# Gate columns of a float32 mixer projected on the split operands

## The chip, the cores and the metric

The kernel runs on one core of one Trainium2 chip. The metric is the device time of the whole program in microseconds (us); smaller is better. TensorE (PE in the profile) does the matmuls, VectorE (DVE), ScalarE (ACT) and GpSimd (POOL) the elementwise work, and SyncE (SP) issues the transfers. Each engine works through its own instructions in order, and waits where an operand is not there yet.

## The reference, cut to what matters

Two layers of a diffusion backbone on 2048 latent tokens and 256 context tokens of 1024 channels. Each layer normalises and modulates the tokens, projects them on one weight `w_in` with 4112 columns, and feeds two groups of heads: a gated convolution and a gated delta rule that is scanned in both directions. The last 16 of the 4112 columns are the ones of this document: 8 write gates and 8 decays (2 directions, 4 heads).

```python
mod_l = silu(c) @ w_mod + b_mod                    # shift, scale, gate
hl = rms_norm(xl, norm_w) * (1.0 + scale_l) + shift_l
pl = split_proj(to_scan_order(hl, col_major) @ w_in)   # D_PROJ = 8 * 512 + 16
...
beta = sigmoid(beta_logit)                         # columns 4096 to 4103
g = -exp(a_log) * softplus(alpha_in + dt_bias)     # columns 4104 to 4111
```

All of it is float32.

## The kernel before

**Tiling.** A layer has 18 tiles of 128 tokens, two of context and 16 latent, in five chunks: chunk 0 has two tiles (256 columns), chunks 1 to 4 four each (512 columns). Tokens lie along the free dimension of the matmuls and channels on partitions: `KT` = 8 blocks of 128 channels.

**Operands.** `prep` (L215) makes a chunk's operands, two channel blocks and 256 tokens at a time: PE transposes the normalised tokens (L225), ACT modulates them into the float32 tile `hf` (L231), DVE rounds that to float32r as `hi` (L235), and DVE or POOL takes the rest as `lo` (L236). The tiles are called `h` and `l`, for chunk 0 `hc` and `lc`. The weights are split in the same way into `whi` and `wlo` (L251, L253), and `project` (L278) forms each output as hi\*hi + lo\*hi + hi\*lo in float32r matmuls of 256 columns.

**Gate columns.** The 16 columns do not go that way. `ba_weights` loads them into a tile of 32 columns filled with zeros, `braw`, which has a buffer of its own. `prep` projects `hf` itself on them in full float32, one channel block at a time, each block `k` into one of four column groups of 32 of the array (L240):

```python
for dk in range(2):
    k = k2 + dk
    q = k % 4
    nc.tensor.matmul(acc[32 * q:32 * q + 32, o], bw[:, k, :], hf[:, dk, :], start=(k < 4), stop=(k >= 4))
```

So a chunk has 8 such matmuls for each 256 tokens, 144 in the two layers, and the bank `acc` is held from the first to the last block: a bank of `pt` (two buffers) for chunks 0 to 2, one of `pd` (three buffers, those of `project`) for chunks 3 and 4. `logits` copies the bank to SBUF (L324) and adds the four groups with a matmul per tile on `sel`, four identities on top of each other (L327). `gates` makes write gates and decays of them, which the scan (`delta`) needs.

**Start.** `mod_load` brings eight pieces of `w_mod`, 1 MB each, and `mod_piece` projects both condition vectors on them (L138, in column groups too) and gathers the groups (L143). `vectors` loads the layer's small per-channel vectors into the tile `rows` (L108 to L112), which PE turns channel-major (L114) into `par`. The modulation adds a column of `par` to each piece, so that no `hf` can be made before `par` is there. `rows` is a tile of the tag `dm`, which has three buffers that are handed out in the order of the program text; the tiles `cc` and `cth` of the prologue have that tag too.

**Order.** The text is recorded for all engines and then ordered by a scheduler that simulates the program and picks by priority; `urgent()` raises the priority of operands, weights and consumers by a fixed offset (`HP`). Each engine then runs its list in order. A matmul of the gates, of a scan step or of an operand's transposes stands among the projection's matmuls wherever the scheduler put it. `ba_weights` is not urgent.

## Time and profile before

| | us |
|---|---|
| median of 3 runs | 2879.31 |
| lowest and highest | 2876.04, 2884.07 |
| span of the profiled execution (first to last instruction) | 2868.8 |
| PE busy in it | 2740.4 (96%) |
| DVE, ACT, POOL busy | 1794.5, 1139.6, 1002.2 |

For the profiled execution the span alone is recorded; the median of the runs stands 10.5 us above it, which is the time of the program before its first and after its last instruction, and the spread of the runs. Busy times of PE count the union of records whose ends overlap, since matmuls are pipelined: what a matmul takes of PE is read from its start to the next one's start. A full float32 matmul leaves two records, a float32r matmul one.

### The profile page before, as it was taken

The numbers are of one execution on the slowest core, as the hardware profiler recorded it, in microseconds if no ns is written. First come the engines' busy times: TensorE is split into PE (matmuls) and PEld (weight loads), VectorE is DVE, ScalarE is ACT, GpSimd is POOL, SyncE is SP. The second block draws the span as 40 slices with busy tenths as digits, with TensorE's granted clock in tenths as the row PEclk, the third lists the DMA queues.
The fourth block names the chain that finished last, engine by engine and source line by source line (L and its number), as shares of the span: only waits on it lengthen the run. The fifth ranks groups of instructions, "written<-read, shape, count | busy, mean of one in ns | idle before, by whom it ended". The sixth has DMA issues, their size and how long they took to land. (4 is left out here: it accounts for less than half of the span.)

```text
span 2868.8 us, 62580 instructions
## 1 busy us (share of the span) xinstructions
PE 2740.4 (96%) x23671; PEld 2529.1 (88%) x23671; DVE 1794.5 (63%) x4677; ACT 1139.6 (40%) x2962; POOL 1002.2 (35%) x1354
## 2 busy tenths in 40 slices
PE   7999999999999999999999999999999998999998
PEld 5799899988988999997777998899999888899887
DVE  5686657576586585353246776675766765754765
ACT  3544453533534532232115444435335354322332
POOL 2332322333433343234444222313334333333443
PEclk9999999999999999999999999999999999999999
DMA  8844265553655553347757552545546556434654
GB/s 275 251 120 138 81 174 130 174 162 89 182 145 170 173 139 113 109 149 246 239 161 242 162 144 79 154 112 163 154 115 188 132 168 189 126 116 118 206 173 117
DMA packets 589449, 450.17 MB, mean 157 GB/s; under 512 B 105322, under 2 KB 527196, under 8 KB 589148
## 3 DMA queue, kind: packets, MB, share of 16 engines
q1 hardware_dynamic: 589148, 446.16, 53.7%
q8 instruction: 188, 3.08, 0.4%
q14 instruction: 113, 0.93, 0.1%
HBM read 326.35 MB, written 119.70 MB: 155 GB/s over the span
## 5 line engine op out<-in xcount | busy, mean ns | idle before, releaser
L278 PE MATMUL pd<-h,whi 128*128 128x256 f32 x4096 | 1206.6, 295 | 2.1 <-ACT whi L251 2.1
L278 PE MATMUL pd<-l,whi 128*128 128x256 f32 x4096 | 1207.2, 295 | 0.0
L278 PE MATMUL pd<-h,wlo 128*128 128x256 f32 x4096 | 1199.4, 293 | 0.5 <-POOL wlo L253 0.5
L278 PEld LDWEIGHTS pd<-h,whi 128*128 128x128 f32 x4096 | 795.2, 194 | 11.9 <-issue 6.6
L278 PEld LDWEIGHTS pd<-l,whi 128*128 128x128 f32 x4096 | 795.0, 194 | 9.0 <-issue 5.4
L278 PEld LDWEIGHTS pd<-h,wlo 128*128 128x128 f32 x4096 | 794.8, 194 | 6.4 <-issue 2.9
L253 POOL TENSOR_TENSOR wlo<-raw,whi 128x1024 fp32r<-128x1024 f32 (+1 forms) x148 | 341.3, 2307 | 382.3 <-ACT whi L251 349.7
L899 PE MATMUL pd<-who,yy 128*128 128x512 f32 x1088 | 350.7, 397 | 0.4 <-ACT who L841 0.4
L899 PEld LDWEIGHTS pd<-who,yy 128*128 128x128 f32 x1088 | 203.6, 189 | 48.0 <-ACT yy L874 2.9
L697 ACT ACTIVATE w<-pscan,cs 128x128 f32<-128x128 f32 x272 | 99.5, 367 | 291.8 <-DVE wk L692 209.1
L899 PE MATMUL pd<-wlo,yy 128*128 128x512 f32 x544 | 214.1, 393 | 0.0
L251 ACT CAST whi<-raw 128x1024 fp32r<-128x1024 f32 x148 | 154.7, 1045 | 97.4 <-PE pd L278 60.9
L501 POOL TENSOR_TENSOR nk<-nk,phalf 128x1 f32<-128x1 f32 x144 | 81.7, 567 | 225.2 <-DVE nk L500 205.8
L573 DVE TENSOR_TENSOR tmp<-L,X 64x31 f32<-64x31 f32 (+15 forms) x310 | 127.1, 410 | 39.9 <-DMA L<-blk 25.0
L388 ACT ACTIVATE pd<-y 128x512 f32<-128x512 f32 (+1 forms) x116 | 65.5, 565 | 213.0 <-DVE y L288 200.6
L686 DVE SCALAR_TENSOR_TENSOR r<-pscan,eg,rc 128x128 f32<-128x128 f32 x272 | 93.7, 346 | 76.7 <-PE pscan L684 74.5
L575 DVE TENSOR_TENSOR X<-X,tmp 64x31 f32<-64x31 f32 (+15 forms) x310 | 136.3, 440 | 5.6
L692 DVE TENSOR_SCALAR wk<-pscan,cs 128x128 f32<-128x128 f32 x272 | 93.5, 346 | 69.6 <-PE pscan L689 67.7
L875 POOL TENSOR_TENSOR yy<-ys,yy 128x512 fp32r<-128x512 f32 x68 | 89.9, 1323 | 125.4 <-ACT yy L874 118.3
L660 POOL TENSOR_TENSOR so<-so,mhalf 128x1 f32<-128x1 f32 x136 | 79.2, 590 | 142.5 <-DVE so L659 134.3
L703 DVE SCALAR_TENSOR_TENSOR Sn<-Sn,atot,pscan 128x128 f32<-128x128 f32 x240 | 82.0, 342 | 67.9 <-PE pscan L694 66.6
L874 ACT CAST yy<-ys 128x512 fp32r<-128x512 f32 x68 | 42.1, 619 | 198.2 <-DVE ys L867 136.8
(2212 smaller groups left out, 5317.3 us busy)
## 6 DMA issues: line engine op xcount, KB each, us to landing
raw<-in_w_in_dram SPq DMA_DIRECT2D x148, 512.0 KB, 4.8
rc<-rec_d SPq DMA_DIRECT2D x272, 256.0 KB, 3.1
rec<-rec_d SPq DMA_DIRECT2D x136, 192.0 KB, 2.6
wm<-in_w_mod_dram SPq DMA_DIRECT2D x24, 1024.0 KB, 7.3
rec_d<-y SPq DMA_DIRECT2D x96, 256.0 KB, 2.9
rows<-row_d SPq DMA_DIRECT2D x144, 128.0 KB, 4.1
rec_d<-rec SPq DMA_DIRECT2D x144, 128.0 KB, 4.0
ys<-y_d SPq DMA_DIRECT2D x68, 256.0 KB, 3.5
```

Of the source, the lines that this page charges most:

```text
L251: nc.scalar.copy(hi, raw)
L253: eng.tensor_sub(lo[:, k], raw[:, k], hi[:, k].bitcast(F32))
L278: nc.tensor.matmul(acc[:, c:c + CW], w[i][:, k, :], h[j][:, k, c:c + CW], start=(z == 0), stop=(z == len(passes) - 1))
L501: nc.gpsimd.tensor_tensor(nk[:, i:i + 1], nk[:, i:i + 1], phalf[:, 0:1], ALU.pow)
L573: nc.vector.tensor_tensor(t3, L3[:, j + 1:32, j:j + 1].to_broadcast([2 * nb, m, k]), X3[:, j:j + 1, 0:k].to_broadcast([2 * nb, m, k]), ALU ...
L575: nc.vector.tensor_sub(X3[:, j + 1:32, 0:k], X3[:, j + 1:32, 0:k], t3)
L686: nc.vector.scalar_tensor_tensor(r, p1[:, 0:128], eg[:, g, col], vn, ALU.mult, ALU.subtract)
L692: nc.vector.tensor_scalar(wk, p2[:, 0:128], cs[:, 5 + z0 + d, i:i + 1], None, ALU.mult)
L697: nc.scalar.activation(w, p2[:, 0:128], AF.Copy, scale=cs[:, z0 + d, i:i + 1])
L703: nc.vector.scalar_tensor_tensor(Sn, S, atot[:, g, col], p3[:, 0:128], ALU.mult, ALU.add)
L875: nc.gpsimd.tensor_sub(l_, yr, h_.bitcast(F32))
L899: nc.tensor.matmul(acc, yy[k // 4][:, k % 4, :], wo[k][part][:, cs_], start=(z == 0), stop=(z == 23))
```

## The change

The gate columns are split into two float32r parts like every other weight, and both parts stand side by side in one tile, `two`: for each block `k` 16 columns of the high part and 16 of the low one. Once the operands of a chunk are there, `logits` projects `hi` and `lo` on it, 8 blocks times 2 operands, all summed in one bank: 16 float32r matmuls a chunk, each over all tokens of the chunk. Their stationary operand is 96 columns wide: the 32 that count and the next 64 of the tile, whose sums land on partitions 32 to 95 and are not read. The matmul that gathers the parts then adds the 16 rows of the high part to the 16 of the low one (`both`), from 32 partitions. The bank is of `pd` for all chunks.

The raw columns are now loaded into a tile of tag `dm`. `csil`, the condition vectors, is stored more densely; its matmuls are as many and as large as before. Comments were dropped. Lines below the change stand a few numbers lower or higher: L276, L227 and L140 are the old L278, L225 and L138, L327 is the new projection, L332 the gather.

```diff
+        both = const.tile([32, 16], F32, name="both")
+        nc.vector.tensor_add(both, ident[0:32, 0:16], ident[0:32, 16:32])
...
-        csil = const.tile([128, KT, 32], F32, name="csil")
+        csil = const.tile([128, 2 * KT + 32], F32, name="csil")
...
-                nc.tensor.matmul(acc[32 * q:32 * q + 32, 0:W], csil[:, k, :], wm[:, k, :], start=(r == 0), stop=(r == 1))
+                nc.tensor.matmul(acc[32 * q:32 * q + 32, 0:W], csil[:, 2 * k:2 * k + 32], wm[:, k, :], start=(r == 0), stop=(r == 1))
...
-                for dk in range(2):
-                    k = k2 + dk
-                    q = k % 4
-                    nc.tensor.matmul(acc[32 * q:32 * q + 32, o], bw[:, k, :], hf[:, dk, :], start=(k < 4), stop=(k >= 4))
...
         def ba_weights():
-            raw = wp.tile([128, KT, 32], F32, tag="braw", bufs=1, name="braw")
-            nc.vector.memset(raw, 0.0)
-            nc.sync.dma_start(out=raw[:, :, 0:16], in_=w_in[l][:, 4096:4112].rearrange("(k p) c -> p k c", p=128))
-            return raw
+            raw = dp.tile([128, KT, 16], F32, tag="dm", bufs=3, name="braw")
+            nc.sync.dma_start(out=raw, in_=w_in[l][:, 4096:4112].rearrange("(k p) c -> p k c", p=128))
+            two = wp.tile([128, KT + 2, 32], F32R, tag="two", bufs=1, name="two")
+            nc.gpsimd.memset(two[:, KT:KT + 2, :].bitcast(F32), 0.0)
+            nc.scalar.copy(two[:, 0:KT, 0:16], raw)
+            nc.vector.tensor_sub(two[:, 0:KT, 16:32], raw, two[:, 0:KT, 0:16].bitcast(F32))
+            return two.rearrange("p k c -> p (k c)")
...
-        def logits(acc, ci, small, z_):
+        def logits(h, ci, small, z_):
             g0, n = CHUNKS[ci]
             W = 128 * n
+            acc = pd()
+            for k in range(KT):
+                for j in range(2):
+                    nc.tensor.matmul(acc[0:96, 0:W], bw[:, 32 * k:32 * k + 96], h[j][:, k, :], start=(k + j == 0), stop=(k + j == KT))
             part = stage([128, 512], n)
-            nc.vector.tensor_copy(part[:, 0:W], acc[:, 0:W])
+            nc.vector.tensor_copy(part[0:32, 0:W], acc[0:32, 0:W])
...
-                nc.tensor.matmul(ps[:, 16 * i:16 * i + 16], part[:, 128 * i:128 * i + 128], sel[:, 0:16], start=True, stop=True)
+                nc.tensor.matmul(ps[:, 16 * i:16 * i + 16], part[0:32, 128 * i:128 * i + 128], both[0:32, :], start=True, stop=True)
...
-                    acc = pt() if bank is pidle else pd()
...
-                    logits(acc, p, bank, z_[:, gp - g0:gp - g0 + np_, :])
+                    logits(hs[p], p, bank, z_[:, gp - g0:gp - g0 + np_, :])
```

The scheduler orders the whole program anew. Three places of the built order bear on the prediction.

PE in layer 0, where chunk 3's operands are made beside the projection (L278, `pd<-h,whi` and its like), the operands' transposes (L225) and scan steps (L689 and L712 to L713). Before:

```order
L240 MATMUL pd<-hf,braw 32x256
L278 MATMUL pd<-h,whi 128x256
L278 MATMUL pd<-l,whi 128x256
L240 MATMUL pd<-hf,braw 32x256
L225 MATMUL pt<-ident,xx 128x128 x3
L240 MATMUL pd<-hf,braw 32x256
L225 MATMUL pt<-ident,xx 128x128
L278 MATMUL pd<-h,wlo 128x256
```

And now:

```order
L327 MATMUL pd<-h,two 96x512
L276 MATMUL pd<-h,whi 128x256
L276 MATMUL pd<-l,whi 128x256
L327 MATMUL pd<-l,two 96x512
L327 MATMUL pd<-h,two 96x512
L327 MATMUL pd<-l,two 96x512
L276 MATMUL pd<-h,wlo 128x256
```

Instead of single narrow matmuls between transposes and projections there are runs of full-height ones among the projections, after the chunk's transposes. In the order before, the 144 matmuls of L240 stand in 103 places: 88 alone, 9 times two in a row, twice three, four times eight.

SP at the start, from the third piece of `w_mod` on (`wm`; `xx` and `xs` are token tiles, `raw` weights, `ab` the decay's constants). Before:

```order
L129 DMA wm<-in_w_mod_dram 128x8x256
L108 DMA rows<-in_b_mod_dram 24x128
L109 DMA rows<-in_norm_w_dram 8x128
L110 DMA rows<-in_conv_a_dram 12x128
L111 DMA rows<-in_conv_qkv_dram 36x128
L112 DMA rows<-in_gdn_norm_dram 1x128
L129 DMA wm<-in_w_mod_dram 128x8x256 x5
L169 DMA xx<-in_ctx_dram 128x1024
```

And now:

```order
L131 DMA wm<-in_w_mod_dram 128x8x256 x6
L171 DMA xx<-in_ctx_dram 128x1024
L248 DMA raw<-in_w_in_dram 128x8x128
L171 DMA xx<-in_ctx_dram 128x1024
L248 DMA raw<-in_w_in_dram 128x8x128
L171 DMA xx<-in_x_dram 128x1024 x6
L171 DMA xs<-in_x_dram 128x1024
L311 DMA braw<-in_w_in_dram 128x8x16
L110 DMA rows<-in_b_mod_dram 24x128
L111 DMA rows<-in_norm_w_dram 8x128
```

The five loads of `rows` have moved from behind the third piece of `w_mod` to behind `braw`, the eight loads of tokens with `xs` and the weights.

PE at the start: `csil` are the condition vectors, `acs` the copied groups of a piece. Before:

```order
L138 MATMUL pd<-wm,csil 32x256 x24
L114 MATMUL pt<-ident,rows 128x81
L143 MATMUL pt<-sel,acs 128x2 x4
L138 MATMUL pd<-wm,csil 32x256 x8
L143 MATMUL pt<-sel,acs 128x2 x2
```

And now:

```order
L140 MATMUL pd<-wm,csil 32x256 x48
L227 MATMUL pscan<-ident,xx 128x128 x12
L116 MATMUL pt<-ident,rows 128x81
L145 MATMUL pt<-sel,acs 128x2 x6
L140 MATMUL pd<-wm,csil 32x256 x8
L145 MATMUL pt<-sel,acs 128x2 x2
L140 MATMUL pd<-wm,csil 32x256 x4
```

The transpose of `rows` has moved from behind the third piece of eight matmuls to behind the sixth and behind the first transposes of tokens; all eight gathers (two matmuls each) and two whole pieces now stand behind it.

## Rows read from the trace of the kernel before

**Rows 1.** The page: its head, and the first line of part 1 (busy time of each engine, share of the span, instructions).

```profile
span 2868.8 us, 62580 instructions
PE 2740.4 (96%) x23671; PEld 2529.1 (88%) x23671; DVE 1794.5 (63%) x4677; ACT 1139.6 (40%) x2962; POOL 1002.2 (35%) x1354
```

**Rows 2.** The instructions of line 240: records, shortest, median and longest duration in ns, first and last start in us, shapes.

```profile
L240 PE MATMUL pt<-hf,braw x160: 379/379/404, 53.4 to 1582.0; 128*32 128x256 f32 x160
L240 PE MATMUL pd<-hf,braw x128: 379/379/403, 282.0 to 1781.9; 128*32 128x256 f32 x128
```

**Rows 3.** The timeline of PE around a lone matmul of L240 (start in us, duration in us, engine, line, tiles, shapes, records).

```profile
285.60 0.28 PE L278 MATMUL pd<-l,whi 128*128 128x256 f32 x1
285.72 0.28 PE L278 MATMUL pd<-h,wlo 128*128 128x256 f32 x1
285.93 0.62 PE L240 MATMUL pd<-hf,braw 128*32 128x256 f32 x2
286.48 0.38 PE L278 MATMUL pd<-h,whi 128*128 128x256 f32 x1
286.70 0.28 PE L278 MATMUL pd<-l,whi 128*128 128x256 f32 x1
```

**Rows 4.** The same view: the first run of L240 (eight matmuls), a run of two, and the last run, each with the row behind it.

```profile
53.44 1.07 PE L240 MATMUL pt<-hf,braw 128*32 128x256 f32 x16
54.44 0.39 PE L278 MATMUL pd<-hc,whi 128*128 128x256 f32 x1
...
1541.90 0.62 PE L240 MATMUL pt<-hf,braw 128*32 128x256 f32 x4
1542.46 0.66 PE L225 MATMUL pscan<-ident,xx 128*128 128x128 f32 x4
...
1781.62 0.62 PE L240 MATMUL pd<-hf,braw 128*32 128x256 f32 x2
1782.17 0.39 PE L278 MATMUL pd<-h,whi 128*128 128x256 f32 x1
```

**Rows 5.** The same view of the output projection, whose float32r matmuls have 512 columns.

```profile
1399.75 0.39 PE L899 MATMUL pd<-who,yy 128*128 128x512 f32 x1
1399.98 0.40 PE L899 MATMUL pd<-wlo,yy 128*128 128x512 f32 x1
```

**Rows 6.** The queue of SP at the start: start and duration of the issue in us, and what is loaded. The last row is from the view of transfers: KB and us from issue to landing.

```profile
8.18 2.90 SPq L108 DMA_DIRECT2D rows<-in_b_mod_dram  x1
...
13.56 10.45 SPq L129 DMA_DIRECT2D wm<-in_w_mod_dram  x5
...
38.37 0.33 SPq L169 DMA_DIRECT2D xs<-in_x_dram  x1
...
40.13 0.38 SPq L314 DMA_DIRECT2D braw<-in_w_in_dram  x1
...
braw<-in_w_in_dram SPq DMA_DIRECT2D x1, 64.0 KB, 9.2
```

**Rows 7.** Two stretches of 10 us at the start: length, busy time of PE, PEld, DVE, ACT and POOL with instructions, granted clock, busy share of the transfer engines, GB/s.

```profile
10.00:20.00 10.00, 6.57 (x53) 2.54 (x53) 1.84 (x8) 0.21 (x1) 0.00 (x0) 1.00 0.92 296
20.00:30.00 10.00, 9.82 (x67) 5.86 (x67) 2.41 (x12) 0.00 (x0) 0.00 (x0) 1.00 1.10 348
```

**Rows 8.** The timeline at the start: the transpose of `rows`, one piece of the modulation and the next (PE), the first `hf` (ACT), the first projection, and the first long wait of PE in the projection.

```profile
19.43 0.40 PE L114 MATMUL pt<-ident,rows 81*128 81x81 f32 x1
...
24.14 1.93 PE L138 MATMUL pd<-wm,csil 128*32 128x256 f32 x16
...
26.00 1.01 PE L143 MATMUL pt<-sel,acs 128*128 128x2 f32 x4
...
42.53 1.92 ACT L231 ACTIVATE hf<-pscan,mod,am 128x256 f32<-128x256 f32 x4
...
44.68 0.58 PE L278 MATMUL pd<-hc,whi 128*128 128x256 f32 x1
...
54.67 0.28 PE L278 MATMUL pd<-lc,whi 128*128 128x256 f32 x1
57.65 0.58 PE L278 MATMUL pd<-hc,wlo 128*128 128x256 f32 x1 [2.71 <-DVE wlo L253]
58.03 0.41 PE L278 MATMUL pd<-hc,whi 128*128 128x256 f32 x1
58.25 0.41 PE L278 MATMUL pd<-lc,whi 128*128 128x256 f32 x1
```

**Rows 9.** Waits of PE (line that waited, what ended the wait: us in total, times, longest).

```profile
PE pt L495 <- DMA rec<-rec_d: 20.0, 17, 3.6
PE pt L601 <- DMA tf<-blk: 14.2, 6, 3.4
PE pscan L684 <- DVE Sn L703: 14.0, 15, 2.8
```

**Rows 10.** The timeline of PE around one such wait, and below it the stretch from 226 to 234 us with its granted clock (columns as in the two stretches above).

```profile
225.80 0.28 PE L278 MATMUL pd<-h,wlo 128*128 128x256 f32 x1
229.31 0.32 PE L601 MATMUL pt<-tf,U 32*32 32x32 f32 x4 [3.23 <-DMA tf<-blk]
...
229.94 0.41 PE L278 MATMUL pd<-l,whi 128*128 128x256 f32 x1
230.15 0.41 PE L278 MATMUL pd<-h,wlo 128*128 128x256 f32 x1
...
226.00:234.00 8.00, 4.76 (x79) 4.33 (x79) 1.58 (x3) 4.49 (x11) 0.61 (x2) 0.62 0.63 147
```

More of the change, by code (lines that the diff above doesn't have):

```diff
@@ L102, in hybrid_backbone_kernel @@
         for r in range(2):
-            nc.vector.tensor_copy(csil[:, :, r:r + 1], ps[:, 8 * r:8 * r + 8].unsqueeze(2))
+            nc.vector.tensor_copy(csil[:, r:2 * KT:2], ps[:, 8 * r:8 * r + 8])
     def vectors(l, P):
@@ L213, in prep_load, with prep @@
         return xs
-    def prep(P, xs, n, r, hi, lo, bank, bw, acc, keep):
+    def prep(P, xs, n, r, hi, lo, bank, keep):
         for i in range(0, n, 2):
@@ L761, in prep_pairs @@
                     hs[p] = h_tiles(p)
-                    acc = pt() if bank is pidle else pd()
                     st = early.get(p)
-                    prep(P, prep_load(l, gp, np_, XT[p]) if st is None else st, np_, 0 if p else 1, *hs[p], bank, bw, acc, h_d[p] if p in cl else None)
-                    logits(acc, p, bank, z_[:, gp - g0:gp - g0 + np_, :])
+                    prep(P, prep_load(l, gp, np_, XT[p]) if st is None else st, np_, 0 if p else 1, *hs[p], bank, h_d[p] if p in cl else None)
+                    logits(hs[p], p, bank, z_[:, gp - g0:gp - g0 + np_, :])
                 gates(g0, n, z_[:, 0:n, :], bank)
```

## The prediction

> **What bounds the kernel now.** The page first: PE is busy in 96% of the span and no other engine in more than 63% [rows 1]. So what an instruction takes of PE, from its start to the next one's start, counts nearly in full, and what stands on the other engines counts only where PE waits for it. Then the instructions of line 240: 288 records for 144 matmuls, a record 379 ns long, from 53.4 to 1781.9 us [rows 2]. A duration says little here, since matmuls overlap; the timeline has the price. A projection matmul of 256 columns starts 0.12 us after the one before it. A lone matmul of L240 starts 0.21 us after its predecessor, the next projection 0.55 us later, and the one after that 0.22 us later [rows 3]: 0.98 us from 285.72 to 286.70 where two steps of 0.12 would be without it, so 0.74 us for a lone one, of which 0.09 and 0.10 are lost ahead of it and behind it. Last the start, where PE waits for operands rather than the reverse [rows 6 to 8], and the waits of PE later on [rows 9, 10].
>
> **What is removed.** The built order has 103 runs of L240: 88 of one matmul, 11 of two or three, 4 of eight. A run of two takes 0.56 us from its start to the transpose behind it (1541.90 to 1542.46), a run of eight 1.00 us (53.44 to 54.44), the last lone one 0.55 us again [rows 4]. With the same 0.19 us around each run that is 0.75 us for two and 1.19 us for eight. I take 0.75 for three as well. 88 x 0.74 + 11 x 0.75 + 4 x 1.19 = 65 + 8 + 5 = **78 us** of PE.
>
> Matmuls in different column groups do run beside each other: eight in one run cost 0.15 us each, five times less than a lone one [rows 4]. The Trainium skill, TensorEngine Tiling (Array Packing), Overview, promises up to four times for a stationary operand of 32 columns or fewer, and speaks against giving the groups up. Were all 144 packed in eights, 18 runs would cost 18 x 1.19 = 21 us, less than what replaces them, and the change would be a loss by about 29 us. The order has four such runs of 103, so the sum goes by the lone ones.
>
> **What is added on PE.** Per layer 4 x 16 matmuls of 512 columns and 16 of 256. The trace has float32r matmuls of 512 columns at 0.23 us from start to start, with a weight load before each [rows 5], and of 256 columns at 0.12 us [rows 3]: 128 x 0.23 + 32 x 0.12 = 29 + 4 = **33 us**. That a stationary operand of 96 columns costs what one of 128 does is not in the trace. Below, the bound is the moving columns alone, the same 33 us, since the stream and not the load sets the step here. Above, it is a narrow operand that empties the array like L240: 0.19 us for each of 160, 30 us more. I take 33, nearest to rows of the same type and length; 63 is kept for the range.
>
> The Trainium skill, TensorE: Matmul & The Clock Gate, Back-to-back issue gap, gives about 131 ns for a sustained matmul of 512 columns; by that the 128 would be an estimated 17 us and the sum 12 us better. The output projection of this kernel needs 0.23 us each, and that decides.
>
> The gathers (36 matmuls, in 10 runs of two or four) now read 32 partitions. If that too empties the array on both sides, it is 10 x 0.19 = **2 us**; if not, nothing. I take 2.
>
> **What costs nothing.** The copy of the bank (10 times on DVE), the cast on ACT, the subtraction on DVE and the fill on POOL (twice each) stand beside PE work on engines that are busy 63%, 40% and 35% [rows 1]; they are in place of a copy and two fills. If the cover went they would be under 1 us each at a place where PE waits for `beta`. The bank of `pd` is now held for a run of matmuls instead of a chunk; PE doesn't wait for a bank in the stretches of L240, so I give nothing for it.
>
> **What moves at the start.** This is the one place where the new order costs. `braw` now has tag `dm` and precedes `rows` in the text, is not urgent, and takes the turn ahead of it. The loads of `rows` so stand behind `braw` on SP, that is behind all eight pieces of `w_mod`, two weights and nine tiles of tokens, and the transpose of `rows` stands behind six of the eight pieces on PE. Before, `rows` was issued at 8.18 us, and `xs` and `braw` at 38.37 and 40.13; `braw` landed 9.2 us after its issue, at 49.3 [rows 6]. Without the loads of `rows` ahead, transfers should run earlier by what 10 to 20 us lost against the next stretch, 296 against 348 GB/s [rows 7], 1.5 us. `rows` is small and lands right behind `braw`, at about 48 us. From there everything is in line: transpose and copies, about 1 us; eight gathers of 0.94 us (26.00 to 26.94, less the start of the next piece); two pieces of 1.86 us (24.14 to 26.00) [rows 8]; the last addition and the scale, 1 us. 48 + 1 + 7.5 + 3.7 + 1 = 61 us for the first `hf`, which was at 42.53 us [rows 8], so 18.5 us late. Of the work behind it some is ahead by then: the tokens of two chunks are normalised while PE waits. Before, PE stood still for 2.7 us at 54.9 us because DVE was late with `wlo`, and then ran at 0.22 us a projection instead of 0.12 for a few us [rows 8], together about 4 us, which I take as recovered. Net **15 us**. The bounds: 18.5 us and none recovered; or the pieces behind `rows` at half that cost and twice as much recovered, 5 us.
>
> **The sum.** -78 + 33 + 2 + 15 = -28 us. The span was 2868.8 us [rows 1], so 2841; the median of the runs stands 10.5 us above that span, so **2851 us**.
>
> **What is not in the sum.** All orders of scan steps and projections are dealt anew. PE still waits 20 us in total for `rec`, 14 for the blocks of the inversion, 14 for the scan's state [rows 9], where the order puts a matmul ahead of its operand. Each such wait costs twice: at 225.80 us PE stood 3.2 us, and then took 0.21 us a projection; the granted clock of the 8 us is 0.62, that is part of it at the lower level, 1.2 GHz, where the steps are nearly twice as long [rows 10]. With some 1.5 us for that, a wait of this kind is worth 4.7 us. Nothing in the diff adds or takes one by intent, so the sum has none; four more or four fewer are 19 us and belong in the range.
>
> **The rivals.**
>
> The late start is made up in full: the scheduler's later waits have slack, or `rows` lands earlier. For it: PE has waits at 54.9 us to fill. Against it: it is PE that is late, and PE has 96%. The time is 2851 - 15 = 2836.
>
> The new order waits more, and the change loses. The mechanism is the one of [rows 10]: a scan or inversion matmul that comes up on PE before its transfer has landed, with the projections queued behind it. The price is 4.7 us each. From eight more on (38 us) the gain of 28 is gone and the kernel is slower by 9 us or more; ten more give 2898. For it: by the built order the context's inversion now starts some 40 us of PE work earlier, when the start's transfers are not long over. Against it: the kinds of wait and the kinds of work are the same as before, and the order behind the start keeps their pattern.
>
> The new matmuls cost more than the rows say: the narrow stationary operand empties the array each time, 63 us instead of 33, so 2881, no change. For it: L240 does it. Against it: the row of L114, which has 81 columns of output, gives its part of the array as 81*128, the full width, where L240 has 128*32 [rows 2, 8]; 96 should go like 81.
>
> The change doesn't do what it says, in the part that matters: the removed matmuls were in cover of waits of PE. For it: PE is idle for 128 us of the span [rows 1]. Against it: the lone one in the timeline stands between projections that follow at 0.12 us [rows 3]. If a third of the 78 us is cover, 2877, no change.
>
> **How the numbers follow.** A measurement tells 0.3% here, 8.6 us, so faster means under 2871 and slower over 2888. Forecast (2851, itself within 2838 to 2868 by three or four waits more or fewer): 0.58. Start made up, 2836: 0.13. Fewer waits as well as that, about 2825: 0.05. Narrow operand, 2881: 0.06. Cover, 2877: 0.08. More waits, 2898: 0.10. The first three are faster, 0.76; 0.14 the same; 0.10 slower. The range for 8 in 10 runs from 2828 to 2882: it takes in the first two cases and the two without change, and leaves out most of the third and the last.
>
> **What would show it.** In the changed profile: L327 at about 0.23 us from start to start beside projections of 0.12, with no lost 0.1 us around a run; 160 records of it, and none of the removed line. The transpose of `rows` (L116) at about 48 us instead of 19.43, the first `hf` at about 61 instead of 42.53, and PE through chunk 0 about 15 us later than before. If L116 comes at 30 us, the start is wrong. If waits of PE for `rec`, the blocks and the state add up to far more than the 48 us of [rows 9], the new order decides and not the matmuls. If the stretches of layer 1 with operands being made are not shorter than before by some 20 us, the removed matmuls were cover.

## The result, and the profile after

The changed kernel takes 2899.47 us in the median of 5 runs (2892.23 to 2906.44); the kernel before, run beside it, 2876.04 (2873.98 to 2884.07). The ratio is 1.007, with a 95% interval of 1.005 to 1.009: **slower by 0.7%**, where 2851 and a gain were forecast, and outside the range.

The head of the page and its first line, of the changed kernel:

```profile
span 2904.7 us, 62373 instructions
PE 2712.1 (93%) x23543; PEld 2544.2 (88%) x23543; DVE 1790.9 (62%) x4678; ACT 1137.4 (39%) x2964; POOL 998.0 (34%) x1356
```

Against [rows 1], PE is busy 28.3 us less, and it stands idle (span less busy time) 192.6 us instead of 128.4. The matmuls did give time back; 64.2 us of new waiting took it and more. A page shows one execution, here one 7.0 us above the median for the changed kernel and one 5.5 us below it for the kernel before, so some 12 us of the difference between the two pages is chance. (Of the 10.5 us between span and median of the kernel before only some 1.7 are time outside the span, by 2906.44 against 2904.7 us in the changed one; the rest was spread.)

The new matmuls themselves cost what was forecast. The timeline of PE around a run of them (columns as in [rows 3]):

```profile
314.22 0.28 PE L276 MATMUL pd<-h,wlo 128*128 128x256 f32 x1
314.33 0.40 PE L327 MATMUL pd<-h,two 128*96 128x512 f32 x1
...
315.03 0.39 PE L327 MATMUL pd<-l,two 128*96 128x512 f32 x1
315.26 0.39 PE L327 MATMUL pd<-h,two 128*96 128x512 f32 x1
315.49 0.28 PE L276 MATMUL pd<-h,whi 128*128 128x256 f32 x1
315.61 0.28 PE L276 MATMUL pd<-l,whi 128*128 128x256 f32 x1
```

A step of 0.23 us inside the run, 0.11 before it and 0.23 and 0.12 behind it: nothing is lost around the run, as it was around L240 in [rows 3]. The 160 matmuls take 35.6 us from start to start in all.

The start, in the timeline (SPq: the issue of a transfer; in brackets how long the engine had waited, and for what):

```profile
41.21 0.38 SPq L311 DMA_DIRECT2D braw<-in_w_in_dram  x1
42.53 2.22 SPq L110 DMA_DIRECT2D rows<-in_b_mod_dram  x1
...
51.18 0.37 PE L116 MATMUL pt<-ident,rows 81*128 81x81 f32 x1 [6.63 <-DMA rows<-in_conv_qkv_dram]
...
64.67 2.38 ACT L233 ACTIVATE hf<-pscan,mod,am 128x256 f32<-128x256 f32 x5 [13.02 <-DVE am L152]
...
66.52 0.56 PE L327 MATMUL pd<-hc,two 128*96 128x256 f32 x1
66.88 0.63 PE L276 MATMUL pd<-hc,whi 128*128 128x256 f32 x2
```

`rows` is behind `braw` on SP, as the order said. The first `hf` is 22 us later than in [rows 8] and so is the first projection.

Then the place where the context's inversion (L500, L516) and the operands of the next chunks meet. Timeline of PE:

```profile
118.75 0.66 PE L227 MATMUL pscan<-ident,xx 128*128 128x128 f32 x4 [0.19 <-ACT hf L233]
121.51 0.70 PE L516 MATMUL pt<-rec 128*128 128x256 f32 x2 [2.11 <-DVE U L517]
...
130.37 1.06 PE L332 MATMUL pscan<-both,hf 32*128 32x16 f32 x8 [0.81 <-DVE hf L329]
131.36 1.09 PE L227 MATMUL pscan<-ident,xx 128*128 128x128 f32 x8
133.31 0.66 PE L227 MATMUL pscan<-ident,xx 128*128 128x128 f32 x4 [0.86 <-DVE g_z L335]
135.08 0.66 PE L227 MATMUL pscan<-ident,xx 128*128 128x128 f32 x4 [1.11 <-ACT hf L233]
135.99 0.66 PE L227 MATMUL pscan<-ident,xx 128*128 128x128 f32 x4 [0.26 <-ACT hf L233]
143.12 0.90 PE L500 MATMUL pt<-ident,rec 128*128 128x128 f32 x3 [6.48 <-DMA rec<-rec_d]
```

From the gather at 130.37 on no projection stands between these rows. PE has nothing in line but urgent work whose operands are not there: a gather, transposes, the inversion. The same in stretches (columns as in [rows 7]), of the changed kernel and, in the second fence, of the kernel before where the same inversion and transposes stand, there among projections:

```profile
117.00:131.00 14.00, 10.89 (x71) 8.85 (x69) 10.30 (x27) 8.20 (x27) 6.75 (x7) 1.00 0.99 321
131.00:144.00 13.00, 4.30 (x28) 3.32 (x28) 7.13 (x15) 4.43 (x11) 3.66 (x2) 0.75 0.97 311
```

```profile
106.00:120.00 14.00, 14.00 (x106) 11.76 (x105) 8.53 (x18) 7.47 (x20) 4.79 (x5) 1.00 1.06 342
120.00:133.00 13.00, 13.00 (x80) 8.95 (x81) 7.25 (x16) 6.40 (x17) 2.01 (x4) 1.00 0.82 245
```

PE was full there before. Now it is busy 4.30 of 13 us, and the granted clock falls to 0.75, so that part of the stretch is at the lower level of 1.2 GHz.

Last the waits of PE. The three kinds of [rows 9], and below them what the transposes of the operands waited for (us, times):

```profile
PE pt L500 <- DMA rec<-rec_d: 28.0, 19, 6.5
PE pt L606 <- DMA tf<-blk: 14.7, 7, 4.2
PE pscan L689 <- DVE Sn L708: 12.2, 14, 3.3
```

```profile
its engine sat idle before it (us, times) until:
  DVE xx L214: 11.7, 2
  ACT hf L233: 9.2, 18
  DVE g_z L335: 0.9, 1
```

The same of the kernel before:

```profile
  DVE xx L212: 2.2, 1
  DVE xs L212: 0.7, 1
  ACT hf L231: 0.2, 1
```

The three kinds add up to 54.9 us, 6.7 more than before. The transposes waited 21.8 us, against 3.1 in the kernel before; of that the wait for `hf`, that is for ACT to free a bank, was 9.2 against 0.2.

### The profile page after: what moved, and what is told of

It is laid out like the page before. It is cut to its first block, busy times and chain, and to the rows that moved or that the text cites. A ratio compares the mean times of both kernels' runs of the same rounds, so it can differ in the third digit from the quotient of the medians.

```text
span 2904.7 us, 62373 instructions
## 1 busy us (share of the span) xinstructions
PE 2712.1 (93%) x23543; PEld 2544.2 (88%) x23543; DVE 1790.9 (62%) x4678; ACT 1137.4 (39%) x2964; POOL 998.0 (34%) x1356
## 4 chain that ended last, share of the span: by engine, by line
PE 59%; DVE 16%; DMA 15%; issue 4%; ACT 3%; SPq 2%; POOL 1%; POOLq 0%; ACTq 0%; DVEq 0%
PE pd L276 33%; PE pd L903 11%; DVE X L580 3%; DMA rec_d<-rec 3%; DVE tmp L578 2%; DMA rec<-rec_d 2%; DMA L<-blk 2%; PE pscan L694 2%; PE pscan L689 2%; PE pscan L717 1%; PE pt L516 1%; PE pscan L699 1%; PE pscan L718 1%; PE pt L500 1%; DVE y L285 1%
## 5 line engine op out<-in xcount | busy, mean ns | idle before, releaser
L276 PE MATMUL pd<-h,whi 128*128 128x256 f32 x4096 | 1207.3, 295 | 5.2 <-DVE y L394 2.7
L276 PE MATMUL pd<-h,wlo 128*128 128x256 f32 x4096 | 1204.5, 294 | 2.5 <-POOL wlo L251 2.5
L276 PE MATMUL pd<-l,whi 128*128 128x256 f32 x4096 | 1202.7, 294 | 0.0
L276 PEld LDWEIGHTS pd<-h,whi 128*128 128x128 f32 x4096 | 797.0, 195 | 10.3 <-ACT whi L249 3.2
L276 PEld LDWEIGHTS pd<-h,wlo 128*128 128x128 f32 x4096 | 795.8, 194 | 6.5 <-POOL wlo L251 2.9
L276 PEld LDWEIGHTS pd<-l,whi 128*128 128x128 f32 x4096 | 796.6, 194 | 3.8
L249 ACT CAST whi<-raw 128x1024 fp32r<-128x1024 f32 x148 | 154.8, 1047 | 118.9 <-PE pd L276 89.8
L903 PEld LDWEIGHTS pd<-wlo,yy 128*128 128x128 f32 x544 | 102.9, 189 | 20.0
```

The source lines that it names most:

```text
L249: nc.scalar.copy(hi, raw)
L276: nc.tensor.matmul(acc[:, c:c + CW], w[i][:, k, :], h[j][:, k, c:c + CW], start=(z == 0), stop=(z == len(passes) - 1))
L903: nc.tensor.matmul(acc, yy[k // 4][:, k % 4, :], wo[k][part][:, cs_], start=(z == 0), stop=(z == 23))
```

## The experiments

Eighteen kernels ran, each beside the kernel before (medians 2871.6 to 2881.1 us in the five groups); ratios are to that. The theories grew on the way:

- **A**: the late `rows`, and what follows from them, made the loss.
- **B**: the removed matmuls stood where PE has little else to do.
- **C**: the new order waits more, wherever it is dealt anew. C' and C'' are two forms of it: the order of before is a lucky draw, or an average one.
- **D**: the gate matmuls stood between the transposes and covered their waits.
- **E**: the bank decides. Before, the sum's bank was taken ahead of a chunk's transposes and held; the change takes one of `project`'s `pd` banks behind them.

### 1 to 3: the buffer, the late rows, the place of the matmuls

**Experiment 1**, the changed kernel with the raw gate columns in a buffer of their own, so that `rows` comes early again:

```diff
-            raw = dp.tile([128, KT, 16], F32, tag="dm", bufs=3, name="braw")
+            raw = wp.tile([128, KT, 16], F32, tag="braw", bufs=1, name="braw")
```

> The changed kernel, with the raw gate columns in a buffer of their own again, so that the loads of rows stand behind the third piece of w_mod as before. Theory A (the late rows made the loss, and the waits that followed in the first 200 us are its consequence): the first hf is back at about 42 us and the whole gain of the matmuls shows, about 2833 us, 43 below the kernel before. Theory B (the removed matmuls stood in stretches where PE has too little else to do): the start is back, 20 us below the changed kernel, but no more than 10 below the kernel before, 2866 to 2880. Theory C (the new order waits more, wherever it is dealt): anywhere from 2860 to 2895, with waits of PE spread over the whole span.

Measured: 2883.49 us, ratio 1.0041 (1.002 to 1.0063). The first `hf` was back at 42.08 us, and yet PE did not go on:

```profile
43.13 1.12 PE L227 MATMUL pscan<-ident,xx 128*128 128x128 f32 x4 [0.21 <-ACT hf L233]
53.21 0.53 PE L327 MATMUL pd<-hc,two 128*96 128x256 f32 x1 [8.97 <-DVE two L315]
53.54 0.41 PE L327 MATMUL pd<-lc,two 128*96 128x256 f32 x1
53.75 0.41 PE L327 MATMUL pd<-hc,two 128*96 128x256 f32 x1
...
56.74 0.41 PE L276 MATMUL pd<-hc,whi 128*128 128x256 f32 x1
```

All 16 new matmuls of chunk 0 stand ahead of the first projection on PE, and they wait 8.97 us for `two`. The first projection starts at 56.7 us instead of 44.7. Theory A falls as the whole cause.

**Experiment 2**, the kernel before with late rows: its gate columns come through a tile of the same kind.

```diff
-            nc.sync.dma_start(out=raw[:, :, 0:16], in_=w_in[l][:, 4096:4112].rearrange("(k p) c -> p k c", p=128))
+            col = dp.tile([128, KT, 16], F32, tag="dm", bufs=3, name="bcol")
+            nc.sync.dma_start(out=col, in_=w_in[l][:, 4096:4112].rearrange("(k p) c -> p k c", p=128))
+            nc.scalar.copy(raw[:, :, 0:16], col)
```

> The kernel before, its gate columns brought through a tile of tag dm and copied into the padded tile: the late rows alone, full float32 matmuls kept. Theory A: 20 us or more slower than the kernel before, 2896 to 2916, with the first hf at about 64 us. Theory B: the same 20 us in the start, since PE has nothing to fill it with, 2896. Theory C (the start has little to do with it): within 8 us of the kernel before.

Measured: 2912.49 us, ratio 1.0143 (1.0096 to 1.0189). The first projection is 23 us late and the last output projection 42. The 23 are the late start by itself; the other 19 arise later, and experiments 4 and 8 show what a kernel loses there without any late start.

**Experiment 3**, experiment 1 with the new matmuls in `prep`, behind the split of every two channel blocks (288 of 256 columns), and with the bank taken ahead of the chunk, as in the kernel before:

```diff
+                for k in range(k2, k2 + 2):
+                    for j, h in enumerate((hi, lo)):
+                        nc.tensor.matmul(acc[0:96, o], bw[:, 32 * k:32 * k + 96], h[:, k, o], start=(k + j == 0), stop=(k + j == KT))
...
+                    acc = pt() if bank is pidle else pd()
```

> The kernel with the own buffer, and the new matmuls not in a run at the end of a chunk but behind each two channel blocks, with 256 columns each (288 of them at 0.12 us, 35 us in place of 33). If the run at the chunk's end delays the gates or holds a bank at a bad time, this one is faster than the own buffer alone by more than 8 us. Theories A and B: within 8 us of it. Theory C: another deal of the order, up to 20 us either way.

Measured: 2864.96 us, ratio 0.9971 (0.995 to 0.9991): faster than both. It is 18.5 us faster than experiment 1, more than the 8 us that A and B leave room for.

### 4 and 8: what a new deal alone costs

The kernel before with one neutral edit; no matmul is added or removed. Experiment 4 has `k2 == 4`, experiment 8 `k2 == 2`:

```diff
-                (nc.gpsimd if k2 == 6 else nc.vector).tensor_sub(lo[:, k2:k2 + 2, o], hf, h_.bitcast(F32))
+                (nc.gpsimd if k2 == 4 else nc.vector).tensor_sub(lo[:, k2:k2 + 2, o], hf, h_.bitcast(F32))
```

> The kernel before, with one neutral edit: of the four subtractions that make the lower split part, POOL takes the third instead of the fourth. No matmul is added or taken away, but the order on all engines is dealt anew. Theory C (any new deal moves the time, whatever it is for): 15 us or more away from the kernel before, in either direction, through waits of PE that sit at other places. Theory D (the loss of the changed kernel comes from what was removed: the gate matmuls stood between the transposes of the operands and covered their waits, so that the transposes now wait themselves): a neutral deal stays within 10 us of the kernel before, and its transposes take about 39 us of PE as before, not the 70 us that they take in the changed kernel.

Measured: 2914.17 us, ratio 1.0118 (1.0086 to 1.0149). The page:

```profile
span 2912.4 us, 62552 instructions
PE 2746.4 (94%) x23671; PEld 2532.3 (87%) x23671; DVE 1803.1 (62%) x4677; ACT 1139.7 (39%) x2962; POOL 1002.8 (34%) x1354
```

6 us more busy and 38 us more idle than in [rows 1], for an edit that moves one subtraction to another engine.

> The kernel before with POOL taking the second of the four subtractions instead of the fourth: a second neutral deal. In the fourth experiment such a deal cost 34 us, with 38 us more of gaps on PE and 42 us more at the lower clock. Theory C' (the order of before is a lucky draw; any change of the source loses some 25 to 45 us by a new draw, whatever it is for): 2900 to 2925, ratio 1.007 to 1.016. Theory C'' (draws scatter around the kernel before, and the fourth experiment was an unlucky one): 2860 to 2890.

Measured: 2903.51 us, ratio 1.0094 (1.0071 to 1.0117). C' holds for both deals tried: the order of the kernel before is better than its neighbours by 0.9 and 1.2%.

### 5 to 7: leaving matmuls out

**Experiment 5**, the kernel before with half its gate matmuls:

```diff
-                    nc.tensor.matmul(acc[32 * q:32 * q + 32, o], bw[:, k, :], hf[:, dk, :], start=(k < 4), stop=(k >= 4))
+                    if k < 4:
+                        nc.tensor.matmul(acc[32 * q:32 * q + 32, o], bw[:, k, :], hf[:, dk, :], start=True, stop=True)
```

> The kernel before, with half of its gate matmuls left out (the four channel blocks from the fifth on are not projected on the gate columns, so the gates are those of half the channels): 72 of 144 matmuls in column groups fewer. Priced as in the prediction they are half of 78 us, 39 us; in the rows of PE they stand with half of 60, 30 us. If the price counts (no cover), 30 to 39 us faster than the kernel before. Theory D: the transposes then take clearly more of PE than the 39 us of before, 50 or more, and the time falls by less than 20 us. Theory C: as the price, give or take 15 us, with the transposes at 39.

Measured: 2851.01 us, ratio 0.9902 (0.9878 to 0.9926), 28 us under the kernel before, and some 49 under the mean of its three deals (1.0071). The price of 39 lies between; in one order of its own, this can't be told more closely. The transposes take 41.7 us of PE, not 50 or more: against D.

**Experiments 6 and 7** leave out 14 of every 16 new matmuls, 6 from experiment 3 and 7 from experiment 1:

```diff
+                        if k == 0:
...
+                if k == 7:
```

> The third experiment (raw gate columns in a buffer of their own, new matmuls spread behind the split of every two channel blocks) with 14 of every 16 gate matmuls left out, so that the gates are those of one channel block: 252 matmuls of 256 columns fewer. Their price is 252 x 0.12 = 30 us, and in its rows of PE they take 35 us. If the price counts, 30 to 35 us faster than the third experiment, about 0.986 of the kernel before. Theory D: the transposes go back up from 39 us towards 70, and the time falls by 15 us or less, about 0.992 or above. Theory C: anything within 15 us of the price, the transposes at 39.

> The first experiment (raw gate columns in a buffer of their own, 16 new matmuls in a row behind a chunk) with 14 of every 16 gate matmuls left out, so that the gates are those of one channel block: 140 matmuls fewer, 33 of the 37 us that they take in its rows. Theory D: here the transposes already come bunched and wait (69 us); they stay at about 70, and of the 33 us most counts, 20 us or more faster than the first experiment, about 0.996 of the kernel before. If the row of 16 itself covered waits (of the next chunk's tokens, of the banks), less than 15 us. Theory C: 33 us give or take 15.

Measured: 0.9857 (0.981 to 0.9904) and 1.0025 (1.0004 to 1.0046). In the spread kernel the 252 matmuls are worth 1.14% of 2876, 33 us, their full price, give or take 15 by the two intervals; in the one with the row 0.16%, 5 us of 33. The pages of 6 and then of 7:

```profile
span 2849.2 us, 62120 instructions
PE 2694.3 (95%) x23419; PEld 2530.6 (89%) x23419; DVE 1796.9 (63%) x4678; ACT 1139.1 (40%) x2964; POOL 1000.3 (35%) x1356
```

```profile
span 2901.8 us, 62055 instructions
PE 2703.6 (93%) x23403; PEld 2534.1 (87%) x23403; DVE 1789.5 (62%) x4678; ACT 1136.6 (39%) x2964; POOL 1000.3 (34%) x1356
```

Almost the same work, and 154.9 against 198.2 us of idle PE (the executions on the pages lie 10 and 19 us above the medians). D would have had the gaps in both, since the cover is gone in both. They differ in the bank, and in the blocks that are kept, the first and the last, and with them in the place. This made theory E.

### 9 to 14: the same kernels in other deals

The edit of experiment 4 or 8 in the changed kernel (9 and 11), the spread one (10 and 12) and experiment 1 (13 and 14).

> The changed kernel under the same edit as in the fourth experiment (POOL takes the third subtraction). If what the change does is hidden by the draw (theory C'), the changed kernel beats the kernel before under the same edit (2914): work on PE is 55 us less and the late start costs some 22, so 2870 to 2900. Theory D (bunched transposes wait, whatever the draw): transposes at 60 us or more here too, and the time stays at 2890 or above. If the change loses under every deal, 2930 or more.

> The third experiment (own buffer, new matmuls spread) under the same edit. Theory C': its third experiment was already a new draw, so another one moves it by 15 us either way: 2850 to 2885, in any case 30 us or more below the kernel before under this edit (2914). Theory C'' with a lucky third experiment: 2885 to 2905. Transposes at 39 to 45 us in both.

> The changed kernel under the edit of the eighth experiment (POOL takes the second subtraction). Theory C': 2870 to 2900 and below the kernel before under the same edit; theory D: transposes at 60 us or more and 2890 or above; if the change loses under every deal, 2920 or more.

> The third experiment (own buffer, new matmuls spread) with POOL taking the second subtraction: the deal in which the kernel before stands at 1.0094 and the changed one at 1.0088. If the spread kernel gains what its two other deals gain (0.9971 and 0.9952, that is 30 to 48 us under the changed kernel in the same deal), 0.993 to 1.000 here. If those two were good draws, 1.003 or above. Gaps around the transposes under 12 us in either case.

> The first experiment (own buffer, 16 matmuls in a row behind a chunk) with POOL taking the third subtraction. It differs from the changed kernel in that deal (1.0042) by the buffer alone, and from the spread one (0.9952) by the row alone. Late rows cost what the start shows, 10 to 20 us: 0.997 to 1.001, if the draws allow it to be seen. Gaps around the transposes 25 us or more, as in all kernels with the row; under 12 if it was the late rows that made them.

> The same under the other deal (POOL takes the second subtraction; changed kernel 1.0088): 1.002 to 1.006 if late rows cost 10 to 20 us, and gaps around the transposes 25 us or more; 0.995 if the row of 16 cost nothing.

Measured: 9: 1.0042 (1.0022 to 1.0061). 10: 0.9952 (0.9934 to 0.997). 11: 1.0088 (1.0066 to 1.011). 12: 0.9919 (0.989 to 0.9948). 13: 1.0031 (1.0011 to 1.0051). 14: 1.0071 (1.0047 to 1.0095). The table below puts them together. In deal 1 the changed kernel beats the kernel before (1.0118), as C' has it, with 44 us less work on PE (2702.7 against 2746.4) and not the 55 that were expected; in deal 2 it is level with it (1.0094) and not below. 10 and 12 came as expected. 13 and 14 are above what was expected for late rows of 10 to 20 us (1.001 and 1.006 at most): the buffer alone brings less. The gaps around the transposes, 26 and 30 us, are not due to the late rows.

### 15: ACT's pace

Experiment 1 with every second modulation on DVE:

```diff
+                    if dk:
+                        nc.vector.tensor_scalar(hf[:, dk, :], p_, a_, m_, ALU.mult, ALU.add)
+                    else:
+                        nc.scalar.activation(hf[:, dk, :], p_, AF.Identity, scale=a_, bias=m_)
```

> The first experiment, with every second modulation (the one that frees a bank of transposes) made on DVE instead of ACT, so that a group of four transposes waits for 0.3 us of work on each of two engines instead of 0.53 us on one. If the pace of ACT makes the transposes wait in the kernels with a row of 16, the gaps around them go from 28 to 15 us or less, and the steps of 0.53 us between groups of four to 0.36. If they wait for tokens and buffers of earlier work, the gaps stay at 25 or more. The time: between 2850 and 2900, since it is a new deal too.

Measured: 1.0077 (1.0053 to 1.0101). The transposes now wait 11.9 us for DVE's half of `hf` instead of 7.4 us for ACT's, and the gaps behind them (from a transpose's end to the next start on PE, where over 0.15 us) are 30.1 us in all, against 28.2 in experiment 1. But the edit made no hand-over faster. DVE's half takes 0.54 us (shortest, median and longest in ns):

```profile
L234 DVE TENSOR_SCALAR hf<-pscan,am,mod x40: 521/540/548, 43.7 to 1597.4; 128x256 f32<-128x256 f32 x40
```

That is as long as ACT's 0.56 and not the 0.3 that was expected, and where eight or more transposes stand in a row, four of them take 0.92 us in the median, against 0.91 in experiment 1 and 0.44 in the kernel before. So whether ACT's pace makes the transposes wait once they are bunched stays open.

### 16 to 18: the row with the old bank

Experiment 1 in the three deals, with the bank taken where it was before the change:

```diff
-            acc = pd()
...
+                    acc = pt() if bank is pidle else pd()
                     prep(P, prep_load(l, gp, np_, XT[p]) if st is None else st, np_, 0 if p else 1, *hs[p], bank, h_d[p] if p in cl else None)
```

> The first experiment (own buffer, 16 new matmuls in a row behind a chunk) with one thing put back as it was before: the bank for the sum is taken ahead of the chunk's transposes and held through the chunk, and where no scan runs it is one of the two pt banks, not one of the three pd banks. Theory D (the row itself costs, because matmuls between the transposes covered their waits): as the first experiment, about 1.004, gaps around the transposes 25 us or more. Theory E (the bank decides: taken late and from pd, it puts the row ahead of projections that could run and leaves both pt banks to the inversion, which comes up too early): as the third experiment, 0.993 to 0.999, first projection at 45 us, gaps around the transposes under 12 us.

> The same with POOL taking the third subtraction: own buffer and row gave 1.0031 there, the spread matmuls 0.9952. Theory D: 1.001 to 1.005 and gaps of 25 us or more; theory E: 0.992 to 0.998 and gaps under 12 us.

> The same with POOL taking the second subtraction: own buffer and row gave 1.0071 there, the spread matmuls 0.9919. Theory D: 1.004 to 1.010 and gaps of 25 us or more; theory E: 0.990 to 0.997 and gaps under 12 us.

Measured: 1.0003 (0.9987 to 1.0019), 0.9992 (0.9972 to 1.0012) and 0.9952 (0.9931 to 0.9973). The start of 16 in the timeline of PE:

```profile
44.49 0.79 PE L276 MATMUL pd<-hc,whi 128*128 128x256 f32 x2
...
53.51 0.36 PE L326 MATMUL pt<-hc,two 128*96 128x256 f32 x1 [0.35 <-DVE two L315]
53.70 0.28 PE L326 MATMUL pt<-lc,two 128*96 128x256 f32 x1
```

With the old bank the same row stands behind projections, and its operand is there when its turn comes: 0.35 us of waiting instead of 8.97. And the waits of the transposes:

```profile
its engine sat idle before it (us, times) until:
  ACT hf L233: 3.7, 10
  DVE xx L214: 2.2, 1
  DVE g_z L334: 0.7, 1
```

E also said that the late bank leaves both `pt` banks to the inversion, which takes its own from there, and brings it up too early. The stretches from the start of the span to the first matmul of the inversion show it (columns as in [rows 7], the clock not to be compared, as said at the end; the kernel before, the changed one, experiments 1 and 16):

```profile
0.00:112.30 112.30, 90.12 (x609) 67.11 (x610) 67.27 (x166) 50.65 (x100) 35.15 (x35) 0.98 0.85 264
0.00:95.90 95.90, 52.62 (x364) 40.46 (x364) 39.99 (x112) 30.97 (x57) 21.28 (x28) 0.72 0.70 219
0.00:81.50 81.50, 54.30 (x380) 41.75 (x381) 40.71 (x118) 30.02 (x58) 20.03 (x27) 0.94 0.80 254
0.00:122.90 122.90, 97.46 (x700) 81.83 (x701) 70.21 (x176) 56.29 (x113) 36.96 (x37) 0.99 0.87 272
```

PE has done 90 us of work by then in the kernel before, 53 and 54 with the late bank, and 97 with the old one. Whether the early inversion costs more, or the row ahead of the projections, was not separated.

E holds in part: most of the way from experiment 1 to 3 is the bank, and a rest is the row. The first projection is at 44.5 to 45.1 us in all three, as E had it, instead of 56.7 to 57.4; of the times, 16 and 17 lie between the ranges of D and E, and 18 is in that of E. The gaps behind the transposes, counted as in experiment 15, are 14 to 20 us, between the 26 to 31 of the kernels with the late bank and the 7 to 9 of the spread ones.

### All deals together

Each cell: ratio to the kernel before, and idle time of PE in us (span less busy time of its page).

| | deal 0 | deal 1 | deal 2 | mean | PE busy, mean |
|---|---|---|---|---|---|
| before | 1, 128.4 | 1.0118, 166.0 | 1.0094, 150.9 | 1.0071, 148.4 | 2744.4 |
| changed | 1.007, 192.6 | 1.0042, 182.0 | 1.0088, 195.6 | 1.0067, 190.1 | 2709.3 |
| own buffer (1, 13, 14) | 1.0041, 173.2 | 1.0031, 172.8 | 1.0071, 185.5 | 1.0048, 177.2 | 2711.1 |
| and old bank (16 to 18) | 1.0003, 160.2 | 0.9992, 163.5 | 0.9952, 156.3 | 0.9982, 160.0 | 2705.6 |
| and spread (3, 10, 12) | 0.9971, 150.4 | 0.9952, 151.4 | 0.9919, 145.2 | 0.9947, 149.0 | 2708.1 |

PE's busy time falls by 33 to 39 us in every version. What differs is the idle time, and it falls from row to row in the means: by the ratios the buffer is worth 0.19% (5 us; about as much as one ratio is uncertain), the bank 0.65% (19 us; 11, 11 and 34 in the three deals), the spreading 0.35% (10 us; 9 to 12). The idle times are of one execution each, so differences of a few us between them say nothing. The last version keeps the idle time of the kernel before, and its gain is the whole of the busy time: 1.24%, 36 us, by the means. Of the versions that leave no matmul out it is the best, and beats both kernels.

The edit that makes the deals costs nothing by itself: in the four later rows it moves the time by -0.5 to +0.3%, against +0.9 and +1.2% in the kernel before.

Where the idle time lies (means of the three deals, counted in the traces, us; the 1000th matmul of the projection comes 206 to 255 us into the span):

| | idle PE up to the 1000th | behind it | PE work ahead of the inversion |
|---|---|---|---|
| before | 25.4 | 123.0 | 89.8 |
| changed | 60.7 | 129.4 | 52.3 |
| own buffer | 42.0 | 135.2 | 56.2 |
| and old bank | 29.0 | 131.0 | 97.7 |
| and spread | 29.5 | 119.5 | 87.9 |

Of the 42 us that the changed kernel idles more than the kernel before, 35 are at the start. The buffer and the bank bring them back there, the spreading helps later. What is left in deal 0 is that the kernel before idles only 106 us behind that point, and 125 and 138 in its other deals.

## Why the prediction was wrong, point by point

**What is removed and added: right, and a little too large.** The step of 0.23 us held, the operand of 96 columns lost nothing, and the gathers cost 1 us more in all (9.0 against 8.0 from start to start). The sum forecast 78 - 33 - 2 = 43 us for the matmuls; where nothing else is disturbed (spread, over three deals) it is 36. The rivals of the narrow operand and of the cover fall: the first by the timeline, the second by the spread kernel, which loses the removed matmuls, keeps the idle time of the kernel before (149.0 and 148.4) and gains the whole of the busy time; experiments 5 and 6 agree. Against the narrow operand the prediction had taken the row of L114, and misread it: in `81*128` the 81 are rows of the array, and the operand is 128 columns wide. L327's own rows are the first to show one of 96 (`128*96`), so that this rival was set aside rightly, but not for that reason.

The Trainium skill, TensorE: Matmul & The Clock Gate, Back-to-back issue gap, has 131 ns for a matmul of 512 columns in a sustained stream. For L327 the trace has 230 again, and disagrees.

**What costs nothing: here it failed.** "The bank of `pd` is now held for a run of matmuls instead of a chunk; PE doesn't wait for a bank in the stretches of L240, so I give nothing for it." The bank was the largest term left out, 19 us by the means. It wasn't a wait for a bank: which bank the sum takes, and when, decides where the scheduler puts the row. Taken late and from `pd`, it stands ahead of projections that could run, and the inversion comes up 38 us of PE work earlier (52.3 against 89.8 in the means). The prediction had seen that in the built order, in its rival of more waits, and set it aside because "the kinds of wait and the kinds of work are the same as before". Whether the kind of bank or the moment of taking it does this was not separated.

The Trainium skill, Perfetto Trace Analysis, Optimizing Tensor Performance (Matmuls), wants independent groups of matmuls to rotate through different banks. Both versions do that, one with the two `pt` banks in the first chunks and one with the three of `pd`, and here the version with the smaller pool was the faster one; of when a bank is taken the section says nothing.

**The start: the place right, the term not.** `rows` landed later than thought (51.18 for L116 instead of 48), the first `hf` came at 64.67 instead of 61, and the first projection 22.2 us late instead of 18.5. But undoing it brought 5 us by the means, not 15: without late rows the row of 16 stands ahead of the first projection and waits 9 us itself. Two causes covered each other.

**What is not in the sum: here it failed too.** The new deal was entered at nothing, with 19 us to either side, as if the order before were an average draw. Two neutral deals cost 27 and 34 us by their ratios; the kernel before stands 0.71%, 20 us, below the mean of its three. A forecast for a new deal should have begun there. So the gain was used up: by the means, 20 for the draw, 19 for the bank, 10 for the row and 5 for the buffer, less 36 for the matmuls, is 18 us, a ratio of 1.006, where 1.007 was measured. This sum uses the table's own means, so it had to come out; it says how the loss divides, and confirms nothing.

**The rival that came true** is the one of more waits, 2898 us at 0.10. Its time was right by luck, since its mechanism was mostly wrong: the waits that it named, for `rec`, the blocks and the state, grew by 6.7 us. The waits at the start and around the transposes grew instead. Part of its support was right, the early inversion.

**The signs I had named.** A row of L327 at 0.23 us came. L116 late came. The third, layer 1 not shorter, came too: from the 7728th to the 10000th matmul of the projection and output projection it takes 386.3 us, against 386.8 before. I had read that sign as cover. But the same stretch takes 394 and 395 us in the other two deals of the kernel before, 376 in experiment 1, which has the row, and 375 to 381 in the spread kernels, so what hid the gain was again the order. By the means the spread kernels are 13 us shorter there than the kernel before, not the 20 of the sign.

**What stays open.** Why the draw of before is good is not known; only two others were run. The bank's 19 us are a mean of 11, 11 and 34. The 5 us of the buffer (0.29, 0.11 and 0.17% in the three deals) are within the uncertainty of each ratio; the row against the spread (0.32, 0.40 and 0.33%) is above it, but only just.

## What to carry to other kernels

Where a scheduler orders the program, run the kernel before under one or two neutral edits first: their spread is the measure for every change, and a kernel that was kept for its time may sit at its good end. Compare an edit with the old kernel over the same few deals, and split the difference into busy and idle time of the bounding engine, since the first is mostly the edit (a neutral deal moved it by 6 us here) and the second mostly the order. When an accumulation moves, keep its bank and its place in the allocation order until that change has been timed by itself.

## What the runs showed of the hardware

A stationary operand of 96 columns costs what one of 128 does, 0.23 us for 512 float32r columns (L327 above, and [rows 5]).

Waiting also cost clock. With PE busy 4.30 of 13 us the granted clock was 0.75 in the changed kernel. In experiment 1, behind the wait of 8.97 us, it was 0.50 from 53.5 to 56.7 us, the lower level, and a matmul of 256 columns took 0.21 us instead of 0.12.

The clock of a whole span can't be compared here. Its records begin at 14.6 us of the span in the changed kernel's profile, at 50.5 in the kernel before and at 68.3 in experiment 9. Ahead of the first record a view reads 1.00, as from 10 to 30 us in [rows 7], and as from 45 to 50 us of the kernel before, where a projection took 0.21 us all the same. From 70 us on, PE was at the lower level for 103 us with 108 us idle in the kernel before, 145 with 153 in the changed one, and 185 with 171 in experiment 7. It does not go by the amount of idle time alone: experiment 9 had 108 us at the lower level with 143 idle.

The Trainium skill, TensorE: Matmul & The Clock Gate, A second HAM failure mode: psum-queue depth-cycling, tells of short idle times between groups of matmuls that make the clock swing between its two levels. The stretch of the changed kernel has few waits and long ones, up to 6.48 us, so it does not show that case.
